# Token sums of x from the channels-first copy: squares, an addition tree and one product with ones

## The chip, the cores and the metric

One NeuronCore of one Trainium2 chip runs the whole program. The metric is the device time of one execution in microseconds. Three runs of the kernel before took 2039.52, 2042.97 and 2034.0 us; their median is 2039.52 us.

## What is computed

The program is a two-layer encoder trunk on 256 tokens of 2048 channels, all in f32. Each layer normalises its input, multiplies it by one wide matrix, runs four branches on the columns of that product, gates and merges them, and adds the result to the input:

```python
def _rms_norm(t, g):
    tf = t.astype(jnp.float32)
    y = tf * lax.rsqrt(jnp.mean(tf * tf, axis=-1, keepdims=True) + NORM_EPS)
    return (y * g.astype(jnp.float32)).astype(t.dtype)
...
    for l in range(DEPTH):
        h = _rms_norm(x, norm_g[l])
        p = h @ w_in[l]
...
        mem_n = _rms_norm(mem, mem_norm_g[l])
        y_d = _mem_attention(m_q, mem_n, mem_w_kv[l], mem_qk_g[l])
...
        x = x + z @ w_out[l]
```

What matters here is the first line of layer 0: every token of x needs the factor (mean of its squared channels + 1e-6) to the power -1/2, and no product of h with w_in can begin before it.

## The kernel before

**Products.** Every weight matrix is streamed from the chip's memory in pieces of two 128-row blocks, 512 KB, into the tile `raww` (three buffers). Each row block of a piece is split into two parts of fewer bits, `whi` (a copy on ScalarE) and `wlo` (the difference, on VectorE), five buffers each; activations are split likewise into `S` (memory, layer by layer), or `T1h` and `T1l` (the normalised x). Each product on TensorE is the sum of high times high, low times high and high times low. The function `product` (line 602) issues them; all matmuls have line 156 and all ScalarE and VectorE instructions line 95, since helpers record them, so they are told apart by their tiles.

**The order of the work.** `main` (line 542) goes through a fixed list of jobs. In layer 0 the first two are the products of the memory tokens with `mem_w_kv` (tiles `S` times `whi`/`wlo`; results `raw` and `V`), the third is the first product of h with `w_in` (`T1h`/`T1l` times `whi`/`wlo`). Beside it run lanes, generators that are given a turn by a running estimate of each engine's time: `norms`, `prep`, `xs`, the `tables` of positions, and the branches. A scheduler of the compiler then sets the order on each engine by its own estimate of durations and by priorities; `issue_after(...)` adds an order between two instructions. Each engine executes its list strictly in order.

**The opening.** Memory arrives channels-first (`memT`, eight pieces of 256 KB into `U` and `ygh`) on ScalarE's DMA queue, the weights on SyncE's. `tick` (line 213) holds a transfer back: it writes one column of its target on GpSimd behind the i-th memset of a row of memsets (`ticks`, lines 190 to 209, each 0.5 us), and the transfer has to wait for that write.

**x in layer 0.** `x_first` (line 401) waits for the last split of memory. It fetches x twice: channels-first (`xT`, four pieces of 512 KB into the freed `U` and `ygh`), and, in `token_sums` (line 381), tokens-first (`in_x`, two pieces of 1 MB into `Z`). From `Z`, ScalarE takes four sums of squares of 1024 channels each, with the sum kept per token (128 tokens on the partitions, so one or two numbers per partition). `rsqrt` (line 176) then raises 128x2 numbers to the power -0.5 on GpSimd. VectorE spreads each over 128 columns (`sq`), and two transposes on TensorE, through the bank `pa`, turn that into a row per token that is the same in all partitions; ScalarE copies it to `r4` (printed as `r`). VectorE multiplies each of 16 channel blocks by the gain and by `r4`, and ScalarE and VectorE split the results into `T1h` and `T1l`. The same `token_sums` serves the memory tokens afterwards (`mrs`); that stays.

Of the kernel before, what the change touches and what calls it, by code (L numbers as in the profile page):

```python
# [15 lines left out]
AF = mybir.ActivationFunctionType  # L16
ALU = mybir.AluOpType
# [4 lines left out]
L, D, S, BW = 2, 2048, 256, 512  # L22
KT = D // 128
EPS = 1e-6
# [12 lines left out]
HP = 2000  # L37
# [8 lines left out]
XE = 5.0  # L46
# [66 lines left out]
class Builder:  # L113
# [230 lines left out]
    def mem_prep(self, l):  # L344

        nc, a = self.nc, self.a
        T = [self.t(f"S{i}", [128, 4, 256], F32R) for i in range(8)]
        X3 = self.t("U", [128, 3, 4, 256])
        X = [X3[:, j] for j in range(3)] + [self.t("ygh", [128, 4, 256])]
        q = nc.scalar if l == 0 else nc.sync  # L350
        g = self.t("gains", [128, 32])
        with self.tc.high_priority(2 * HP):
            nc.sync.dma_start(g, a["gcols"][l])
        self.v["mT", l] = T
        self.v["gains", l] = g
        mem = a["memT"]

        def load(i):
            dst = X[i // 2][:, i % 2 * 2:i % 2 * 2 + 2]
            if not l and i in (1, 2, 3):  # L360
                self.tick((0, 1, 4, 7)[i], dst[:, 0, 0:1])
            q.dma_start(dst, mem[:, 2 * i:2 * i + 2])

        for i in range(8 if l else 4):
            load(i)
        self.ev.add(("mload", l))
        for i in range(8):
            if not l and 1 <= i <= 4:
                with self.tc.issue_after(self.last[0]):
                    load(i + 3)  # L370
            if not l and i == 3:
                with self.tc.issue_after(self.fetch):
                    nc.sync.dma_start(self.cst, a["consts"])
            for kk in (2 * i, 2 * i + 1):
                j, k = kk // 4, kk % 4
                with self.tc.high_priority(2 * HP if kk < 4 else 0):
                    self.split(T[j][:, k], T[4 + j][:, k], X[j][:, k], scale=g[:, kk:kk + 1])
                self.ev.add(("mT", l, kk))
            yield 0.0
# [21 lines left out]
    def x_first(self):  # L401

        nc, a = self.nc, self.a
        yield from self.until(("mT", 0, 15))
        X3 = self.t("U", [128, 3, 4, 256])
        X = [X3[:, j] for j in range(3)] + [self.t("ygh", [128, 4, 256])]
        for j in range(4):
            with self.tc.issue_after(self.last[0]):
                nc.scalar.dma_start(X[j], a["xT"][:, 4 * j:4 * j + 4])
        rs = self.small(2)  # L410
        yield from self.token_sums(a["x"][0], rs)
        ex = self.t("sq", [128, 2, 128])
        nc.vector.tensor_copy(ex, rs[:, :, None].to_broadcast([128, 2, 128]))
        ps = self.pa()[:, :256]
        for tt in range(2):
            self.tr(ps[:, tt * 128:tt * 128 + 128], ex[:, tt])
        rb = self.t("r4", [128, 256], bufs=1)
        self.copy(rb, ps)
        yield
        g = self.v["gains", 0][:, 16:32]  # L420
        hi = self.t("T1h", [128, 16, 256], F32R)
        lo = self.t("T1l", [128, 16, 256], F32R)
        for j in range(8):
            xs = X[j // 2][:, j % 2 * 2:j % 2 * 2 + 2]
            for k in range(2):
                with self.tc.issue_after(self.last[1]):
                    nc.vector.scalar_tensor_tensor(xs[:, k], xs[:, k], g[:, 2 * j + k:2 * j + k + 1], rb,
                                                   op0=ALU.mult, op1=ALU.mult)
            self.split(hi[:, 2 * j:2 * j + 2], lo[:, 2 * j:2 * j + 2], xs)
            yield  # L430
        self.v["hT", 0] = (hi, lo)
        self.ev.add(("hT", 0))
        mrs = self.t("mrs", [128, 2])
        yield from self.token_sums(a["mem"][0], mrs)
        self.v["mrs"] = mrs
        self.ev.add("mrs")
# [105 lines left out]
    def main(self):  # L542
        nc = self.nc
        jobs = [j for l in range(L) for j in self.jobs(l)]
        chunks = [(j, k0, min(2, j.nk - k0)) for j in jobs for k0 in range(0, j.nk, 2)]
        flat = [(i, k) for i, (j, k0, n) in enumerate(chunks) for k in range(n)]
        raws, parts = {}, {}
        nxt = [0]

        def prepare(upto):  # L550
            while nxt[0] < len(flat) and nxt[0] <= upto:
                i, k = flat[nxt[0]]
                j, k0, n = chunks[i]
                w = j.ncol
                if k == 0:
                    raw = self.t("raww", [128, 2, 512], bufs=3)
                    with self.tc.high_priority(HP):
                        for q, (b, e) in enumerate(((0, 1), (1, 2)) if i < 3 else ((0, n),)):
                            if 2 * i + q in (1, 2, 3, 4, 5):
                                self.tick((0, 0, 3, 4, 5, 6)[2 * i + q], raw[:, q, 0:1])  # L560
                            with self.tc.issue_after(self.fetch) if 0 < i < 5 else nullcontext():
                                self.fetch = nc.sync.dma_start(
                                    raw[:, b:e, :w], j.src.rearrange("(k p) n -> p k n", p=128)
                                    [:, k0 + b:k0 + e, j.c0:j.c0 + w]).ins
                    raws[i] = raw
                hi = self.t("whi", [128, 512], F32R, bufs=self.LOOK)
                lo = self.t("wlo", [128, 512], F32R, bufs=self.LOOK)
                with self.tc.high_priority(HP):
                    self.last = self.split(hi[:, :w], lo[:, :w], raws[i][:, k, :w])
                parts[i, k] = (hi, lo)  # L570
                nxt[0] += 1

        pos = 0
        for i, (j, k0, n) in enumerate(chunks):
            if k0 == 0:
                if j.ready is not None:
                    yield from self.until(j.ready)
                act = j.act()
                banks = {}
            nb = 2 if not j.tpos else (j.ncol + 255) // 256  # L580
            if i and (k0 == 0 or k0 + n == j.nk):
                order = [[(k, b) for k in range(n)] for b in range(nb)]
            else:
                order = [[(k, b) for b in range(nb)] for k in range(n)]
            for step in order:
                for k, b in step:
                    kk = k0 + k
                    prepare(pos + k + self.LOOK - 1)
                    if j.kready is not None:
                        yield from self.until(j.kready(kk))  # L590
                        if kk == j.nk - 1:
                            yield from self.until(j.kready(j.nk))
                    if b not in banks:
                        banks[b] = self.bank("mm", 4)
                    self.product(j, kk, b, banks[b], parts[i, k], act(kk))
                    if kk == j.nk - 1:
                        with self.tc.high_priority(HP):
                            j.evac(b, banks[b])
                yield
            pos += n  # L600
# [947 lines left out]
```

## Time and profile before

| | |
|---|---|
| median of three runs | 2039.52 us (2034.0 to 2042.97) |
| profiled execution | 2035.4 us, of which its span 2033.5 us |
| TensorE busy in the span | 2016.3 us (99%) |
| VectorE, ScalarE, GpSimd busy | 1417.8, 1118.1, 152.9 us |
| TensorE matmuls | 12066 |
| moved | 369.45 MB, mean 182 GB/s |

The profile is that of one execution; its times count from the start of the span. Busy times of TensorE are those of pipelined matmuls. A time in square brackets behind a row of the timeline is how long the engine sat idle before it, and which instruction ended that.

### The profile page before, as it was taken

How to read it: one execution, taken by the hardware profiler on the slowest of the kernel's cores; microseconds unless marked ns; L12 is line 12 of the kernel's file. 1: busy time of each engine (PE TensorE's matmuls, PEld its weight loads, DVE VectorE, ACT ScalarE, POOL GpSimd, SP SyncE). 2: the span in 40 equal slices, each digit the busy share in tenths (PEclk: the TensorE clock that was granted, in tenths of full speed). 3: DMA queues.
4: the chain of work that ended last, by engine and by line, in shares of the span. 5: the costliest groups of instructions: out<-in, count | busy, mean ns of one | idle time of the engine just before them, and what ended most of it. 6: DMA issues, size and time to landing. Idle time of an engine off the chain costs nothing.

```text
span 2033.5 us, 33805 instructions
## 1 busy us (share of the span) xinstructions
PE 2016.3 (99%) x12066; PEld 1695.8 (83%) x12066; DVE 1417.8 (70%) x3070; ACT 1118.1 (55%) x2317; POOL 152.9 (8%) x174
## 2 busy tenths in 40 slices
PE   8999999999999999999999999999999999999999
PEld 6998997887877888777889988888778778877887
DVE  5878888986587577558565658666656876765664
ACT  5756565655455445446465556765555554444543
POOL 1201100210010000000000010110011001000000
PEclk9999999999999999999999999999999999999999
DMA  8665655566455556656765656455555555665565
GB/s 298 215 183 157 189 173 171 148 186 186 141 181 165 169 171 191 198 171 226 237 191 179 182 156 179 147 164 175 161 181 166 176 157 158 197 200 165 183 201 190
DMA packets 222585, 369.45 MB, mean 182 GB/s; under 512 B 40592, under 2 KB 60816, under 8 KB 221840
## 3 DMA queue, kind: packets, MB, share of 16 engines
q1 hardware_dynamic: 218736, 356.31, 57.8%
q10 hardware_dynamic: 3456, 10.49, 1.3%
q8 instruction: 95, 1.56, 0.3%
q0 software_dynamic: 224, 0.49, 0.2%
q14 instruction: 74, 0.61, 0.1%
HBM read 359.88 MB, written 11.53 MB: 183 GB/s over the span
## 4 chain that ended last, share of the span: by engine, by line
PE 91%; issue 3%; DVE 2%; DMA 2%; ACT 1%; SPq 0%; POOL 0%; ACTq 0%; DVEq 0%; POOLq 0%
PE mm L156 81%; PE pr L156 5%; PE pa L156 3%; PE pa L161 2%; DMA raww<-in_mem_w_kv 1%; DVE wlo L95 1%; PE pr L161 0%; DVE S L95 0%; DMA raww<-in_w_in 0%; DMA U<-in_memT 0%; ACT whi L95 0%; SPq L1375 0%; DVE Z L95 0%; DVE BK L95 0%; POOL small L179 0%
## 5 line engine op out<-in xcount | busy, mean ns | idle before, releaser
L95 ACT ACTIVATE whi<-raww 128x512 fp32r<-128x512 f32 (+2 forms) x1300 | 786.7, 616 | 738.3 <-PE mm L156 407.0
L95 DVE TENSOR_TENSOR wlo<-raww,whi 128x512 fp32r<-128x512 f32 (+2 forms) x1300 | 863.9, 675 | 449.7 <-ACT whi L95 439.2
L156 PE MATMUL mm<-wlo,T1h 128*128 128x512 f32 (+2 forms) x1440 | 564.6, 392 | 2.6 <-DVE wlo L95 2.6
L156 PE MATMUL mm<-whi,T1l 128*128 128x512 f32 (+2 forms) x1472 | 566.1, 388 | 0.0
L156 PE MATMUL mm<-whi,T1h 128*128 128x512 f32 (+2 forms) x1472 | 537.7, 391 | 1.3 <-ACT whi L95 1.2
L156 PEld LDWEIGHTS mm<-whi,T1h 128*128 128x128 f32 x1472 | 275.3, 188 | 57.1 <-ACT whi L95 2.1
L156 PEld LDWEIGHTS mm<-whi,T1l 128*128 128x128 f32 x1472 | 276.5, 188 | 51.8 <-issue 0.3
L156 PEld LDWEIGHTS mm<-wlo,T1h 128*128 128x128 f32 x1440 | 270.6, 188 | 57.8 <-DVE wlo L95 5.1
L156 PE MATMUL mm<-T1l,whi 128*128 128x256 f32 x960 | 272.4, 285 | 0.4 <-DVE T1l L95 0.4
L156 PE MATMUL mm<-T1h,wlo 128*128 128x256 f32 x960 | 272.6, 286 | 0.0
L156 PE MATMUL mm<-T1h,whi 128*128 128x256 f32 x960 | 272.5, 285 | 0.0
L156 PEld LDWEIGHTS mm<-T1l,whi 128*128 128x128 f32 x960 | 183.6, 191 | 1.6 <-DVE T1l L95 0.6
L156 PEld LDWEIGHTS mm<-T1h,whi 128*128 128x128 f32 x960 | 183.6, 192 | 1.2
L156 PEld LDWEIGHTS mm<-T1h,wlo 128*128 128x128 f32 x960 | 183.0, 191 | 0.8
L156 PE MATMUL mm<-wlo,ygh 128*128 128x512 f32 (+1 forms) x296 | 116.5, 396 | 0.0
L156 PE MATMUL mm<-whi,ygl 128*128 128x512 f32 (+1 forms) x296 | 115.6, 393 | 0.0
L156 PE MATMUL mm<-whi,ygh 128*128 128x512 f32 (+1 forms) x296 | 110.0, 395 | 0.0
L156 PE MATMUL mm<-whi,S 128*128 128x512 f32 x256 | 86.5, 414 | 5.0 <-ACT whi L95 4.8
L179 POOL TENSOR_TENSOR small<-small,cst 128x4 f32<-128x4 f32 (+3 forms) x46 | 52.3, 1139 | 514.1 <-DVE small L95 430.1
L156 PEld LDWEIGHTS mm<-whi,ygl 128*128 128x128 f32 x296 | 55.6, 188 | 12.3 <-issue 1.0
L156 PEld LDWEIGHTS mm<-whi,S 128*128 128x128 f32 x256 | 50.0, 198 | 19.1 <-ACT whi L95 7.6
L156 PEld LDWEIGHTS mm<-whi,ygh 128*128 128x128 f32 x296 | 55.6, 188 | 12.3 <-issue 1.0
(279 smaller groups left out, 2165.8 us busy)
## 6 DMA issues: line engine op xcount, KB each, us to landing
raww<-in_w_in SPq DMA_DIRECT2D x432, 512.0 KB, 3.6
raww<-in_w_branch SPq DMA_DIRECT2D x64, 512.0 KB, 4.5
raww<-in_w_out SPq DMA_DIRECT2D x64, 512.0 KB, 4.6
raww<-in_mem_w_kv SPq DMA_DIRECT2D x29, 512.0 KB, 3.6
raww<-in_w_in SPq DMA_DIRECT2D x16, 384.0 KB, 3.6
raww<-in_w_in SPq DMA_DIRECT2D x16, 320.0 KB, 3.7
raww<-in_w_in SPq DMA_DIRECT2D x16, 256.0 KB, 2.8
Z<-in_x ACTq DMA_DIRECT2D x2, 1024.0 KB, 6.9
```

The lines of the kernel that those rows point to most:

```text
L95: return g(out, *args, **kw)
L156: return self.nc.tensor.matmul(out, lhsT=lhsT, rhs=rhs, start=start, stop=stop).ins
L161: self.nc.tensor.transpose(out, in_, self.ident[:k, :k])
L179: self.nc.gpsimd.tensor_tensor(ss, ss, self.cst[:, C_MH:C_MH + n], op=ALU.pow)
```

## The change

The tokens-first fetch of x is taken out. ScalarE squares the four channels-first pieces (128x1024 each) into the tile `T1l`, which is not yet in use; VectorE adds pieces 0 and 1, 2 and 3, the two results, and then halves the row twice, until 128x256 is left: for each token a sum over 16 channels in each partition. One f32 product with a 128x128 matrix of ones (tile `Rs`) adds the 128 partitions and leaves in every partition the same row of 256 sums. VectorE scales it and adds the small constant (128x256), and GpSimd raises all 128x256 numbers to the power -0.5, with a tile `sq` that is filled with -0.5 as the exponent. The spreading copy and the two transposes go.

The releases by `tick` move: the second to fourth memory piece from steps 1, 4, 7 to 0, 3, 6, and four of the early weight pieces by one step. Fewer splits of memory have the raised priority in layer 0.

```diff
@@ mem_prep
-                self.tick((0, 1, 4, 7)[i], dst[:, 0, 0:1])
+                self.tick((0, 0, 3, 6)[i], dst[:, 0, 0:1])
...
-                with self.tc.high_priority(2 * HP if kk < 4 else 0):
+                with self.tc.high_priority(2 * HP if kk < (4 if l else 2) else 0):
@@ x_first
-        rs = self.small(2)
-        yield from self.token_sums(a["x"][0], rs)
-        ex = self.t("sq", [128, 2, 128])
-        nc.vector.tensor_copy(ex, rs[:, :, None].to_broadcast([128, 2, 128]))
+
+        sq = self.t("T1l", [128, 4, 1024])
+        one = self.t("Rs", [128, 128], bufs=2)
+        nc.gpsimd.memset(one, 1.0)
+        yield XE
+        for j in range(4):
+            with self.tc.issue_after(self.last[0]):
+                nc.scalar.activation(sq[:, j], X[j].rearrange("p k t -> p (k t)"), AF.Square)
+            if j % 2:
+                with self.tc.issue_after(self.last[1]):
+                    nc.vector.tensor_tensor(sq[:, j - 1], sq[:, j - 1], sq[:, j], op=ALU.add)
+            yield
+        nc.vector.tensor_tensor(sq[:, 0], sq[:, 0], sq[:, 2], op=ALU.add)
+        nc.vector.tensor_tensor(sq[:, 0, 0:512], sq[:, 0, 0:512], sq[:, 0, 512:1024], op=ALU.add)
+        nc.vector.tensor_tensor(sq[:, 0, 0:256], sq[:, 0, 0:256], sq[:, 0, 256:512], op=ALU.add)
         ps = self.pa()[:, :256]
-        for tt in range(2):
-            self.tr(ps[:, tt * 128:tt * 128 + 128], ex[:, tt])
+        self.mm(ps, one, sq[:, 0, 0:256])
         rb = self.t("r4", [128, 256], bufs=1)
-        self.copy(rb, ps)
+        nc.vector.tensor_scalar(rb, ps, 1.0 / D, EPS, op0=ALU.mult, op1=ALU.add)
+        half = self.t("sq", [128, 256])
+        nc.gpsimd.memset(half, -0.5)
+        nc.gpsimd.tensor_tensor(rb, rb, half, op=ALU.pow)
         yield
@@ main, prepare
-                                self.tick((0, 0, 3, 4, 5, 6)[2 * i + q], raw[:, q, 0:1])
+                                self.tick((0, 0, 2, 3, 4, 5)[2 * i + q], raw[:, q, 0:1])
```

The scheduler also moves instructions. On TensorE, at the end of the second product with `mem_w_kv` (bank `mm_403` before, `mm_401` now; `S_8` and `S_12` are the last blocks of memory), stood before:

```order
L156 MATMUL mm_403<-whi_496,S_8_98 128x512
L161 MATMUL pa_489<-cst,sq_487 128x128 x2
L156 MATMUL mm_391<-wlo_497,S_8_98 128x512
...
L156 MATMUL mm_403<-wlo_535,S_8_98 128x512
L156 MATMUL mm_403<-whi_534,S_12_102 128x512
L156 MATMUL mm_649<-T1h_516,whi_550 128x256
L156 MATMUL mm_675<-T1h_516,whi_550 128x256
L156 MATMUL mm_649<-T1l_517,whi_550 128x256
```

and now stands:

```order
L156 MATMUL mm_401<-wlo_534,S_8_98 128x512
L156 MATMUL mm_401<-whi_533,S_12_102 128x512
L156 MATMUL pa_486<-T1l_302,Rs_303 128x256
L156 MATMUL mm_648<-T1h_527,whi_545 128x256
L156 MATMUL mm_674<-T1h_527,whi_545 128x256
L156 MATMUL mm_648<-T1l_528,whi_545 128x256
```

The transposes stood 22 matmuls before the first product with `T1h`; the product with ones stands directly before it, and the third matmul behind it reads `T1l`.

On VectorE, from the end of the token sums to the first `T1l`, stood before (`E` belongs to the tables of positions):

```order
L95 SCALAR_TENSOR_TENSOR U_296<-U_296,gains_105,r_103_492 128x256 x4
L95 SCALAR_TENSOR_TENSOR E_626<-E_626 128x64
L95 TENSOR_TENSOR wlo_561<-raww_548,whi_560 128x512
L95 SCALAR_TENSOR_TENSOR U_296<-U_296,gains_105,r_103_492 128x256 x2
L95 TENSOR_TENSOR wlo_577<-raww_574,whi_576 128x512
L95 TENSOR_SCALAR E_626<-E_626 128x64
L95 TENSOR_TENSOR T1l_517<-U_296,T1h_516 128x512 x2
```

and now stands:

```order
L95 TENSOR_TENSOR T1l_302<-T1l_302 128x256
L95 TENSOR_TENSOR wlo_546<-raww_543,whi_545 128x512
L95 TENSOR_TENSOR wlo_560<-raww_543,whi_559 128x512
L95 TENSOR_TENSOR wlo_572<-raww_569,whi_571 128x512
L95 TENSOR_TENSOR wlo_579<-raww_569,whi_578 128x512
L95 TENSOR_SCALAR r_101_488<-pa_486 128x256
L95 TENSOR_TENSOR wlo_645<-raww_642,whi_644 128x512
L95 SCALAR_TENSOR_TENSOR U_296<-U_296,gains_105,r_101_488 128x256 x12
L95 SCALAR_TENSOR_TENSOR ygh_297<-ygh_297,gains_105,r_101_488 128x256 x4
L95 TENSOR_TENSOR T1l_528<-U_296,T1h_527 128x512 x6
```

The first `T1l` came behind 6 of the 16 multiplications by `r4`; it now comes behind all 16.

On GpSimd, behind the fetch of the gains of the rotary part, stood before:

```order
L246 DMA kkn_449<-in_mla_rope_g 128x128
L179 ISA
L179 TENSOR_TENSOR small_302<-small_302,cst 128x2
L254 TENSOR_TENSOR ropeg_666<-cs,kkn_449 128x2x32 x8
L179 TENSOR_TENSOR mrs_619<-mrs_619,cst 128x2
```

and now stands:

```order
L246 DMA kkn_447<-in_mla_rope_g 128x128
L254 ISA
L254 TENSOR_TENSOR ropeg_665<-cs,kkn_447 128x2x32 x8
L431 TENSOR_TENSOR r_101_488<-r_101_488,sq_490 128x256
L179 TENSOR_TENSOR mrs_618<-mrs_618,cst 128x2
```

The power of 128x2 numbers is replaced by one of 128x256, and it now stands behind the eight products of the rotary tables.

## Rows read from the trace of the kernel before

**Rows 1.** The page, part 1 (busy time) and part 4 (chain of work).

```profile
PE 2016.3 (99%) x12066; PEld 1695.8 (83%) x12066; DVE 1417.8 (70%) x3070; ACT 1118.1 (55%) x2317; POOL 152.9 (8%) x174
...
PE 91%; issue 3%; DVE 2%; DMA 2%; ACT 1%; SPq 0%; POOL 0%; ACTq 0%; DVEq 0%; POOLq 0%
```

**Rows 2.** Stretches: us, busy of PE, PEld, DVE, ACT, POOL; granted clock; DMA share, GB/s.

```profile
32.00:38.00 6.00, 3.97 (x17) 2.63 (x15) 1.39 (x3) 2.99 (x6) 0.00 (x0) 1.00 1.05 415
38.00:43.00 5.00, 3.38 (x13) 2.15 (x14) 1.35 (x3) 2.25 (x5) 0.00 (x0) 1.00 1.01 395
43.00:50.00 7.00, 7.00 (x23) 5.26 (x24) 5.64 (x15) 6.80 (x13) 0.75 (x1) 0.76 0.57 186
...
72.00:140.00 68.00, 68.00 (x569) 67.90 (x569) 57.49 (x111) 44.60 (x102) 11.62 (x12) 1.00 0.57 169
```

**Rows 3.** Chain of waits, 0 to 130 us: start us, us, what.

```profile
29.95 12.22 DMA raww<-in_mem_w_kv
```

**Rows 4.** DMA issues, 24 to 44 us: total, then KB each, median us to landing.

```profile
DMA packets 2538, 7.43 MB, mean 371 GB/s; under 512 B 204, under 2 KB 204, under 8 KB 2279
...
Z<-in_x ACTq DMA_DIRECT2D x2, 1024.0 KB, 6.9
U<-in_xT ACTq DMA_DIRECT2D x3, 512.0 KB, 8.4
```

**Rows 5.** Timeline of TensorE: start us, us, instruction, [idle before].

```profile
9.07 1.22 PE L156 MATMUL mm<-whi,S 128*128 128x512 f32 x2 [0.52 <-ACT whi L95]
...
42.87 0.74 PE L156 MATMUL mm<-whi,S 128*128 128x512 f32 x2 [1.62 <-ACT whi L95]
...
56.42 0.38 PE L161 MATMUL pa<-cst,sq 128*128 128x128 f32 x2
...
61.76 0.40 PE L156 MATMUL mm<-T1h,whi 128*128 128x256 f32 x2
62.10 0.39 PE L156 MATMUL mm<-T1l,whi 128*128 128x256 f32 x1
...
68.47 0.39 PE L156 MATMUL mm<-T1l,whi 128*128 128x256 f32 x1 [0.36 <-DVE T1l L95]
```

**Rows 6.** Timeline of ScalarE in the opening.

```profile
33.56 0.63 ACT L95 ACTIVATE whi<-raww 128x512 fp32r<-128x512 f32 x1 [3.65 <-DMA raww<-in_mem_w_kv]
...
38.30 1.04 ACT L95 ACTIVATE Z<-Z 128x1024 f32<-128x1024 f32 x1
```

**Rows 7.** Timeline of GpSimd: single powers of 8, 2, 1 and 4 columns.

```profile
472.40 1.64 POOL L179 TENSOR_TENSOR small<-small,cst 128x8 f32<-128x8 f32 x1 [20.57 <-DVE small L95]
...
614.94 0.70 POOL L179 TENSOR_TENSOR small<-small,cst 128x2 f32<-128x2 f32 x1 [12.42 <-DVE small L95]
...
1266.80 0.56 POOL L179 TENSOR_TENSOR small<-small,cst 128x1 f32<-128x1 f32 x1 [16.08 <-DVE small L95]
1280.95 1.01 POOL L179 TENSOR_TENSOR small<-small,cst 128x4 f32<-128x4 f32 x1 [13.59 <-DVE small L95]
```

**Rows 8.** Groups of GpSimd by shape: busy us, mean ns of one, idle before.

```profile
L179 POOL TENSOR_TENSOR small<-small,cst 128x4 f32<-128x4 f32 x20 | 21.5, 1077 | 126.6 <-DVE small L95 126.6
L179 POOL TENSOR_TENSOR small<-small,cst 128x8 f32<-128x8 f32 x8 | 16.2, 2025 | 114.1 <-ACT jk L95 62.9 <-DVE small L95 49.4 <-ACT PT L95 1.8
```

**Rows 9.** Timeline of GpSimd: the old power of x, and a multiplication of 256 columns.

```profile
49.20 0.75 POOL L179 TENSOR_TENSOR small<-small,cst 128x2 f32<-128x2 f32 x1 [35.22 <-DVE small L95]
...
753.73 0.78 POOL L1195 TENSOR_TENSOR kds<-kds,r 128x256 f32<-128x256 f32 x1 [16.34 <-DVE r L95]
```

**Rows 10.** Timeline of VectorE: multiplications by `r4` and the first `T1l`.

```profile
61.36 1.29 DVE L95 TENSOR_TENSOR T1l<-U,T1h 128x512 fp32r<-128x512 f32 x2
...
63.17 2.46 DVE L95 SCALAR_TENSOR_TENSOR U<-U,gains,r 128x256 f32<-128x256 f32 x6
```

**Rows 11.** Groups of VectorE by shape, 40 to 110 us.

```profile
L95 DVE TENSOR_SCALAR jk<-E 128x256 f32<-128x256 f32 x4 | 1.4, 360 | 0.0
```

**Rows 12.** Groups of TensorE by shape: f32 products of 256 columns.

```profile
L156 PE MATMUL pr<-LA,aup 128*128 128x256 f32 x32 | 9.5, 379 | 0.0
```

## The prediction

> **What bounds the kernel now.** I read the page first, then the table of stretches for the first 140 us, then the timelines of the engines there. TensorE is busy for 99% of the span and carries 91% of the chain that ended last [rows 1]; from 72 us on it has no gap over whole stretches [rows 2]. So TensorE's list is the bound, and the change is worth what it takes from or adds to TensorE's idle time around the start of layer 0. Nothing later catches such time up: a TensorE that stands still for 10 us at 57 us ends 10 us later.
>
> The opening is another stage. From 32 to 43 us TensorE idles 2.03 + 1.62 = 3.65 us while the DMA engines are full, at about 400 GB/s [rows 2]. What ends the waits is a weight piece of the memory product: the chain follows one for 12.22 us [rows 3], ScalarE waits 3.65 us for one before it can split it [rows 6], and TensorE waits 1.62 us in turn [rows 5]. Afterwards the granted clock averages 0.76 over 7 us [rows 2], a mixture of the levels 1.2 and 2.4 GHz, which loses 0.24 x 7 = 1.7 us of work. From 24 to 44 us 7.43 MB are moved, of which the tokens-first x is two transfers of 1 MB [rows 4]. The squares of x take 1.04 us each and lie beside TensorE's work [rows 6].
>
> **The fetch that goes.** 2.1 MB at 371 GB/s [rows 4] are 5.7 us of full DMA engines, more than the 3.65 us of idle time. I take both the idle time and the lost clock as gone: -3.65 and -1.7 us. At the other end they all stay, since the pieces also queue among themselves: 0.
>
> **The tree.** Four squares stay four, of the same size. Five additions on VectorE, the largest 1024 columns, come beside TensorE's second memory product; VectorE is not full there, and its last addition stands ahead of splits that TensorE uses before it reaches the product with ones. Nothing on the path. If that cover were gone, the last addition of 256 columns would add about as much as a multiplication of 256 columns, 2.46/6 = 0.41 us [rows 10].
>
> **The product and what hangs behind it.** Before, the transposes ran at 56.42 us, 5.3 us before the first product with `T1h` at 61.76 [rows 5], and the spreading and half of the multiplications hid behind those 5.3 us. Now the product with ones stands directly ahead of that first product. TensorE has nothing else in its list, so everything between is idle time of TensorE. Step by step:
>
> - Start of the product: 61.76 - 3.65 - 1.7 - 0.38 for the transposes that go [rows 5] = 56.0 us.
> - The product, two passes of 0.38 [rows 12]: 0.76.
> - VectorE's scaling of 128x256: 0.36, as for such an instruction from the on-chip memory [rows 11].
> - GpSimd's power of 128x256. The trace has no power wider than 8 columns. Undisturbed ones take 0.56, 0.70, 1.01 and 1.64 us for 1, 2, 4 and 8 columns [rows 7]: 0.14 to 0.16 us for each further column, with no flattening. From 2 to 8 columns it is 0.94/6 = 0.157 us, so 256 columns are an estimated 1.64 + 248 x 0.157 = 40.5 us. This is the largest term. Bounds: below, a multiplication of 256 columns on GpSimd took 0.78 us [rows 9]; above, the means of the groups, which hold disturbed ones, rise by (2025 - 1077)/4 = 237 ns per column [rows 8], which gives 60.8 us. I take 40.5: the rows are of the same operation, and the engine that disturbs it, VectorE, has nothing to do meanwhile.
> - All 16 multiplications by `r4`, since the first `T1l` now stands behind all of them: 16 x 0.41 = 6.56 [rows 10].
> - The first `T1l`, half of 1.29: 0.65 [rows 10].
>
> Sum 48.8 us; `T1l` is ready at 104.8, where its first reader ran at 62.10 [rows 5]: +42.7 us. The next seven `T1l` come every 0.6 us, faster than TensorE uses them, so the wait of 0.36 us at 68.47 [rows 5] goes. After so long a stop TensorE starts at the lower clock; I take the 1.7 us that the stop at 42.87 was followed by. **42.7 - 0.4 + 1.7 = +44.0 us.**
>
> The Trainium skill speaks against this reading. Its page GPSIMD Engine Reference, section 3.1, puts a two-input elementwise instruction there at about 2.6 cycles per element of a partition; at its 1.2 GHz that is an estimated 0.55 us for 256 columns. The multiplication of 0.78 us agrees [rows 9]; the powers do not [rows 7], and with 0.55 in place of 40.5 the change would be about +4 us.
>
> **Queues.** On GpSimd the power now stands behind eight rotary products. They wait for a table that VectorE's new order has ahead of the second memory product's first split, over 15 us before; eight of them are done by then. Behind the power waits the power of the memory sums, whose readers are ScalarE's scalings of the memory results; they move with the rest. On ScalarE the `T1h` copies and the next weight splits queue behind the wait; on SyncE the weight pieces stop once three buffers are full. All of that idles along with TensorE and costs nothing more. The releases by `tick` come one memset, 0.5 us, earlier; TensorE's idle time of 0.52 us at 9.07 [rows 5] may shrink or grow by that. I put it at 0, between -1 and +1.
>
> **From one execution to the median.** The profiled execution took 2035.4 us, so the sum gives 2079.4. It lies 4.1 us under the median of the runs; the mean of the three runs and of this one is 2038.0, and 2038.0 + 44.0 = **2082 us** is the forecast. A measurement of this kernel can tell about 0.5%, 10 us, from no change.
>
> **Rivals.**
>
> 1. *The power is cheap* (0.78 us, like the multiplication [rows 9], and as the page of the Trainium skill would have it). Then the idle time between the product and `T1l` is 9.1 us and the sum +4.3: 2042 us, no change where I forecast slower. It decides if the power takes under 40.5 - (44.0 - 10.2) = 6.7 us, that is 0.024 us per column. For it: a long instruction may be worked off in blocks that 8 columns do not fill. Against it: then 1, 2, 4 and 8 columns should cost nearly the same, and they don't [rows 7]. Chance 0.12; in 0.02 of it the opening gains so much more that the time is faster by over 0.5%.
> 2. *The opening gains nothing* (the weights stay late, because the earlier releases and the four x pieces of 512 KB, 8.4 us each [rows 4], fill the queue anyway). The power costs 40.5 and the 5.3 us stay: 2087 us. For it: ScalarE's waits are for weights, not for x [rows 6]. Against it: the engines are full, and 2.1 of 7.43 MB go. Chance 0.10.
> 3. *The power is dearer*, 60.8 us by the means [rows 8]: 2102 us. Against it: disturbed powers only. Chance 0.06.
>
> **How the numbers follow.** The forecast has 0.72. The low end takes the smallest step between widths, 0.14 us from 1 to 2 columns (0.70 + 254 x 0.14 = 36.3, -4.2), no loss of clock (-1.7) and a run like the lowest (-4): 2072, and 2071 with the early releases at their best. The high end takes rival 2 (+5.3), a run like the highest (+5) and some more at the lower clock: 2095. That leaves out rivals 1 and 3, 0.18 together. Slower by over 0.5%: 0.72 + 0.10 + 0.06 = 0.88; within: 0.10; faster: 0.02.
>
> **What would show it.** GpSimd has one instruction on 128x256 from `r` and `sq` to `r`, starting near 57 us, of about 40 us; TensorE stands still between the product with ones and the first `T1l` for about 48 us, then runs at the lower clock for a few us; the idle time from 32 to 43 us is gone and the product with ones starts near 56 us; from there to the end the stretches are as before, only later. The prediction is wrong if the power takes under 7 us, or if TensorE has other matmuls to run during it.

## The result, and the profile after

The changed kernel takes 2095.88 us (median of 4 runs, 2093.14 to 2097.06), the kernel before beside it 2038.22 us (4 runs): a ratio of 1.028, 95% interval 1.0255 to 1.0306. It is slower by 57.7 us, where 44 were forecast; the range ended at 2095. The profiled execution took 2095.46 us, its span 2093.7 us.

The page of the changed kernel, parts 1 and 4, against [rows 1]:

```profile
PE 2029.8 (97%) x12066; PEld 1689.9 (81%) x12066; DVE 1426.0 (68%) x3072; ACT 1120.6 (54%) x2312; POOL 184.9 (9%) x176
...
PE 88%; DMA 3%; DVE 3%; POOL 2%; issue 2%; ACT 1%; SPq 0%; DVEq 0%; ACTq 0%; POOLq 0%
```

GpSimd is busy 32 us more and appears in the chain with 2%. TensorE is busy for 97% of a longer span; its busy time, too, has grown, by 13.5 us with the same number of matmuls.

Stretches of the changed kernel (columns as in [rows 2]):

```profile
32.00:43.00 11.00, 9.68 (x41) 7.27 (x40) 9.16 (x18) 8.90 (x14) 1.64 (x5) 1.00 0.71 263
43.00:55.60 12.60, 12.60 (x55) 10.19 (x55) 9.73 (x15) 6.31 (x12) 0.00 (x0) 1.00 0.79 239
62.00:97.00 35.00, 0.00 (x0) 0.00 (x0) 0.00 (x0) 0.00 (x0) 35.00 (x1) 0.50 0.03 13
...
105.00:110.00 5.00, 4.88 (x23) 4.88 (x24) 4.83 (x9) 0.76 (x2) 0.00 (x0) 0.50 0.04 7
110.00:116.00 6.00, 6.00 (x49) 6.00 (x49) 2.81 (x5) 4.09 (x7) 0.00 (x0) 0.94 0.55 168
```

From 32 to 43 us the idle time of TensorE is 1.3 us in place of 3.65 [rows 2], and the clock stays at the full level afterwards. From 62 to 97 us one GpSimd instruction runs and nothing else does. After the stop the granted clock is 0.50 until about 110 us.

TensorE's timeline (as [rows 5]), then the chain of waits through the stop:

```profile
35.72 0.74 PE L156 MATMUL mm<-whi,S 128*128 128x512 f32 x2 [1.32 <-ACT whi L95]
55.60 0.59 PE L156 MATMUL pa<-T1l,Rs 128*128 128x256 f32 x2
99.64 0.80 PE L156 MATMUL mm<-T1h,whi 128*128 128x256 f32 x2 [43.44 <-ACT T1h L95]
105.12 0.58 PE L156 MATMUL mm<-T1l,whi 128*128 128x256 f32 x1 [4.68 <-DVE T1l L95]
```

```profile
56.74 41.28 POOL r L431
98.02 0.02 issue
98.04 4.84 DVE U L95 x12
102.88 1.58 DVE ygh L95 x4
104.46 0.61 DVE T1l L95
105.07 0.04 issue
105.12 30.95 PE mm L156 x238
```

The product with ones starts at 55.60 (56.0 in the prediction), the power takes 41.3 us (40.5), the first `T1l` is read at 105.12 (104.8). At this point the change has cost 105.12 - 62.10 = 43.0 us. But the cost goes on growing. One power of 128x4 stands once in each of eight head groups; here are the first and the last of them in the kernel before and in the changed one:

```profile
138.20 1.45 POOL L1123 TENSOR_TENSOR small<-small,cst 128x4 f32<-128x4 f32 x1 [44.61 <-DVE small L95]
...
1709.73 1.01 POOL L1123 TENSOR_TENSOR small<-small,cst 128x4 f32<-128x4 f32 x1 [6.84 <-DVE small L95]
```

```profile
182.05 1.45 POOL L1136 TENSOR_TENSOR small<-small,cst 128x4 f32<-128x4 f32 x1 [50.57 <-DVE small L95]
...
1764.36 1.01 POOL L1136 TENSOR_TENSOR small<-small,cst 128x4 f32<-128x4 f32 x1 [6.77 <-DVE small L95]
```

The distance is 43.9 us at the first, 54.6 at the last, 60.2 at the ends of the spans. Some 16 to 17 us come after the stop, in small pieces. TensorE waits no more than before there, but is busy for longer. Here is the stretch from the first `T1l` to its last matmuls, before and after (columns as in [rows 2]):

```profile
62.10:2028.00 1965.90, 1959.11 (x11859) 1653.12 (x11859) 1379.78 (x2981) 1081.93 (x2249) 144.02 (x144) 1.00 0.59 179
```

```profile
105.12:2088.00 1982.88, 1976.51 (x11858) 1650.48 (x11859) 1374.87 (x2958) 1078.69 (x2238) 131.37 (x136) 1.00 0.58 176
```

The idle time is 6.8 us before and 6.4 after; the busy time has grown by 17.4 us for the same work, of which the lower clock behind the stop has 2.8 (see below). The groups of matmuls by shape (busy us, mean ns) show the rest, first before, then after:

```profile
L156 PE MATMUL mm<-whi,T1l 128*128 128x512 f32 x1344 | 524.4, 394 | 0.0
...
L156 PE MATMUL mm<-whi,k 128*128 128x512 f32 x64 | 21.6, 396 | 0.0
...
L156 PE MATMUL mm<-whi,q 128*128 128x512 f32 x64 | 21.2, 392 | 0.0
```

```profile
L156 PE MATMUL mm<-whi,T1l 128*128 128x512 f32 x1344 | 530.2, 398 | 0.0
...
L156 PE MATMUL mm<-whi,k 128*128 128x512 f32 x64 | 21.6, 395 | 0.0
...
L156 PE MATMUL mm<-whi,q 128*128 128x512 f32 x64 | 21.2, 392 | 0.0
```

At the same granted clock the matmuls of 512 columns with `T1l` take 4 ns longer, those with `k` and `q` do not. The time from the start of one matmul to the start of the next, called the pitch here, was worked out from all starts of such matmuls in the trace (gaps over 300 ns left out): its median rises from 227 to 234 ns and its mean from 228.3 to 233.1. There are about 4,000 with `T1h` or `T1l`, so 4.8 x 4,000 = 19 us. The 2,880 of 256 columns, which read `T1h` and `T1l` as the moving operand, get faster, from a median of 120 to 117 ns; by the means (123 to 121.5) that is some 5 us. Together +14 us.

What differs is where the tiles lie. The changed `x_first` asks for `T1l` before all others and for `Rs` early, so that the allocation shifts: within 512 bytes of a partition, `T1h`, `T1l` and `V1` start at 0x1a0 (bytes, hexadecimal) in the kernel before and at 0x180, 32 bytes lower, in the changed one. `whi` and `wlo` start at 0x1a0 in both. These places are read off the built programs, no profile shows them; whether they are the cause was for the runs.

### The profile page after: what moved, and what is told of

Its sections match the earlier page's. It is cut to its first block, busy times and chain, and to the rows that moved or that the text cites. A ratio compares the mean times of both kernels' runs of the same rounds, so it can differ in the third digit from the quotient of the medians.

```text
span 2093.7 us, 33802 instructions
## 1 busy us (share of the span) xinstructions
PE 2029.8 (97%) x12066; PEld 1689.9 (81%) x12066; DVE 1426.0 (68%) x3072; ACT 1120.6 (54%) x2312; POOL 184.9 (9%) x176
## 4 chain that ended last, share of the span: by engine, by line
PE 88%; DMA 3%; DVE 3%; POOL 2%; issue 2%; ACT 1%; SPq 0%; DVEq 0%; ACTq 0%; POOLq 0%
PE mm L156 79%; PE pr L156 5%; PE pa L156 3%; POOL r L431 2%; PE pa L161 2%; DVE wlo L95 1%; DMA sp<-sc 1%; DMA sc<-S 1%; DVE S L95 1%; DMA U<-in_memT 1%; PE pr L161 0%; DMA raww<-in_w_in 0%; ACT whi L95 0%; DMA raww<-in_mem_w_kv 0%; DVE Z L95 0%
## 5 line engine op out<-in xcount | busy, mean ns | idle before, releaser
L156 PE MATMUL mm<-whi,T1l 128*128 128x512 f32 (+2 forms) x1472 | 572.0, 392 | 0.0
L156 PE MATMUL mm<-whi,T1h 128*128 128x512 f32 (+2 forms) x1472 | 543.8, 395 | 1.2 <-ACT whi L95 1.2
L156 PEld LDWEIGHTS mm<-wlo,ygh 128*128 128x128 f32 x296 | 55.7, 188 | 12.2 <-issue 0.7
```

What stands on the lines that cost most here:

```text
L156: return self.nc.tensor.matmul(out, lhsT=lhsT, rhs=rhs, start=start, stop=stop).ins
```

## The experiments

**The places of the tiles put back.** Two unused tiles, nothing else:

```diff
@@ x_first
+        self.t("pada", [128, 8])
         sq = self.t("T1l", [128, 4, 1024])
@@ tables
+        self.t("padb", [128, 120])
         ang = self.t("E", [128, 512], bufs=2)
```

> The changed kernel with two unused tiles in between, of 32 and 480 bytes per partition, so that T1h, T1l and V1 start again at the same place within 512 bytes as in the kernel before (0x1a0 in place of 0x180); every instruction stands in the same order on every engine. Theory 1 (the place of these tiles sets the pitch of the matmuls that read them as the stationary operand): the 512-column matmuls with T1h and T1l go back from 234 to 227 ns from start to start, and the time falls by 15 to 17 us to 2079 to 2081 us; the power still takes 41 us. Theory 2 (the drift after 140 us comes from the scheduler's new order, or is the difference between two executions): the time stays at 2094 to 2098 us and the pitch at 234 ns.

It took 2084.18 us (4 runs), 1.0211 times the kernel before beside it (1.019 to 1.0232; that one took 2041.48 here). The power still takes 41.27 us. The same two instructions of the head groups, then the group of matmuls:

```profile
181.20 1.45 POOL L1138 TENSOR_TENSOR small<-small,cst 128x4 f32<-128x4 f32 x1 [51.27 <-DVE small L95]
...
1754.52 1.01 POOL L1138 TENSOR_TENSOR small<-small,cst 128x4 f32<-128x4 f32 x1 [6.84 <-DVE small L95]
```

```profile
L156 PE MATMUL mm<-whi,T1l 128*128 128x512 f32 x1344 | 525.0, 394 | 0.0
```

The mean is 394 ns again (the pitch 227), and the distance to the kernel before is 43.0 us at the first group, 44.8 at the last and 46.7 at the ends of the spans: most of the growth is gone. In the ratio it is 0.7% of the time, some 14 us; against the changed kernel's median it is 11.7, since this kernel ran beside runs that were 3 us longer. Either is less than the 15 to 17 expected. Theory 2, which had the time unchanged, falls.

**The change's places given to the kernel before.**

```diff
@@ x_first
         self.copy(rb, ps)
+        self.t("pada", [128, 120])
@@ tables
+        self.t("padb", [128, 8])
         ang = self.t("E", [128, 512], bufs=2)
```

> The kernel before with two unused tiles of 480 and 32 bytes per partition, so that T1h, T1l and V1 start at 0x180 within 512 bytes as in the changed kernel, and all else as before; every instruction stands in the same order. Theory 1: the pitch of the 512-column matmuls with T1h and T1l rises from 227 to 234 ns and the time by 15 to 17 us, to 2053 to 2055 us. Theory 2: the time stays at 2034 to 2043 us, the pitch at 227 ns.

2053.31 us (5 runs), a ratio of 1.0062 (1.0043 to 1.0082), beside the same 2041.48: 12 to 13 us for two unused tiles. That is less than the 15 to 17 expected; I think I had left out part of what the 256-column matmuls give back (their median is 117 ns here), but no run shows that alone.

```profile
L156 PE MATMUL mm<-whi,T1l 128*128 128x512 f32 x1344 | 530.1, 398 | 0.0
```

**Which place counts.** In the kernel before, `whi`, `wlo` and `raww` alone moved by 32 bytes:

```diff
@@ main, prepare
+                    if i == 0:
+                        self.t("pad0", [128, 8])
                     raw = self.t("raww", [128, 2, 512], bufs=3)
@@ params
+        if l == 0:
+            self.t("pad1", [128, 120])
         cols = self.t("cols", [128, P_N + 29])
```

> The kernel before with raww, whi and wlo moved by 32 bytes (whi and wlo start at 0x1c0 within 512 bytes in place of 0x1a0), T1h, T1l, V1 and all other tiles at the places they had within 512 bytes; every instruction in the same order. Theory 1a (what counts is the distance between the two operands of a matmul; it is then that of the changed kernel, 0x20): the 512-column matmuls with T1h and T1l take 234 ns from start to start, those of 256 columns 117, and the time rises by about 12 us to 2050 to 2056 us. Theory 1b (the place of the stationary operand alone counts): the 512-column ones stay at 227 ns and the time within 5 us of the kernel before's.

2053.12 us (4 runs), ratio 1.006 (1.0045 to 1.0075), where the kernel before took 2041.19.

```profile
L156 PE MATMUL mm<-whi,T1l 128*128 128x512 f32 x1344 | 530.2, 398 | 0.0
...
L156 PE MATMUL mm<-whi,q 128*128 128x512 f32 x64 | 21.5, 396 | 0.0
...
L156 PE MATMUL mm<-whi,k 128*128 128x512 f32 x64 | 21.3, 392 | 0.0
```

`T1l` and `q`, which lie where they lay, became slow, and `k` became fast, though it did not move either. So the distance between the two operands counts (theory 1a), not the place of one. It is that of the changed kernel: `T1l` starts 32 bytes below `whi`. `k` starts at 0xc0, `whi` now at 0x1c0: for `k`, 256 bytes apart is as good as 0.

**All stationary tiles at distance 0.** In the kernel before, three unused tiles bring `S0` to `S7`, `X`, `ygh` (0x120 before), `ygl`, `k1` and `iA` (0xc0) to 0x1a0:

```diff
@@ setup
+        self.t("pad0", [128, 32])
         pace = self.t("X", [128, 1024])
@@ tables
+        self.t("pad1", [128, 96])
         pp = self.t("q1", [128, 1024], I32)
...
+        self.t("padb", [128, 56])
         ang = self.t("E", [128, 512], bufs=2)
```

> The kernel before with unused tiles in between, so that every tile that a 512-column matmul reads as the stationary operand (S0 to S7, X, ygh, ygl, k1, iA beside T1h, T1l, V1, q1) starts at 0x1a0 within 512 bytes, as whi and wlo do; every instruction in the same order. Both forms of theory 1: the matmuls with S, X, ygh, ygl, k and iA, some 1,500 that take 230 to 233 ns, come down to about 227 to 228, and the time falls by 5 to 8 us to 2030 to 2034 us. Rival (only T1h, T1l and V1 are sensitive, or ygl and ygh take 231 ns for another reason): the time stays within 2 us of the kernel before's.

2037.46 us (12 runs) against 2041.19 (26 runs), ratio 0.9979 (0.9969 to 0.9989): 4.3 us faster by the ratio, a little under the forecast 5 to 8 and more than the rival's 2.

```profile
L156 PE MATMUL mm<-whi,k 128*128 128x512 f32 x64 | 21.3, 391 | 0.0
L156 PE MATMUL mm<-whi,q 128*128 128x512 f32 x64 | 21.1, 391 | 0.0
L156 PE MATMUL mm<-whi,X 128*128 128x512 f32 x64 | 20.9, 391 | 0.0
```

**The power alone.** The changed kernel with the power of 2 columns in place of 256:

```diff
-        nc.gpsimd.tensor_tensor(rb, rb, half, op=ALU.pow)
+        nc.gpsimd.tensor_tensor(rb[:, 0:2], rb[:, 0:2], half[:, 0:2], op=ALU.pow)
```

> The changed kernel with the power taken of 2 of the 256 columns alone; the other 254 columns of the factor are left without it. The order of the instructions is the same but for that one. Theory 1 (the power is the stall): it takes 0.7 us in place of 41.3, TensorE waits 7 to 9 us between the product with ones and the first T1l, and the time falls by 40 to 42 us to 2054 to 2056 us. Rival (another instruction, such as the 16 multiplications or a late weight piece, would hold TensorE anyway): the time falls by less than 30 us.

2055.99 us (4 runs): 39.9 us under the changed kernel's median, and 1.0072 times the kernel before (1.0048 to 1.0096), where the changed kernel is at 1.028; by the ratios that is 42 us. GpSimd, then TensorE:

```profile
57.01 0.72 POOL L431 TENSOR_TENSOR r<-r,sq 128x2 f32<-128x2 f32 x1 [22.20 <-DVE r L95]
```

```profile
59.63 0.50 PE L156 MATMUL mm<-T1h,whi 128*128 128x256 f32 x2 [3.16 <-ACT T1h L95]
65.11 0.58 PE L156 MATMUL mm<-T1l,whi 128*128 128x256 f32 x1 [4.99 <-DVE T1l L95]
```

The power was the stop: the first `T1l` is read at 65.11 in place of 105.12 us. What is left of it, 3.16 + 4.99 us, is the chain of the other steps between the product with ones and the first `T1l`.

**The releases.** The changed kernel with the old steps and the old priority, first in a single execution, then in four:

```diff
-                self.tick((0, 0, 3, 6)[i], dst[:, 0, 0:1])
+                self.tick((0, 1, 4, 7)[i], dst[:, 0, 0:1])
@@ main, prepare
-                                self.tick((0, 0, 2, 3, 4, 5)[2 * i + q], raw[:, q, 0:1])
+                                self.tick((0, 0, 3, 4, 5, 6)[2 * i + q], raw[:, q, 0:1])
@@ mem_prep
-                with self.tc.high_priority(2 * HP if kk < (4 if l else 2) else 0):
+                with self.tc.high_priority(2 * HP if kk < 4 else 0):
```

> The changed kernel with the releases at their old steps and the old priority of the splits of memory, the rest as in the change. Theory 1 (the opening is faster because the tokens-first x is gone): the idle time of TensorE from 32 to 43 us stays near 1.3 us, the product with ones starts within 1 us of 55.6 us, and the time is within 2 us of the changed kernel's. Rival (the earlier releases gave the 5 us): the product starts at 58 us or later.

> The changed kernel with the old releases and the old priority once more, timed in rounds. If the look before holds (product with ones at 59.0 in place of 55.6 us), it starts after 58 us again and the time is 3 to 4 us over the changed kernel's 2095.9, 2098 to 2101 us; if that was the accident of one execution, it starts near 56 us and the time is within 2 us of 2096.

The product with ones started at 59.03 us in the first trace and at 58.55 in the second, so 3 us later than in the change, both times:

```profile
58.55 0.59 PE L156 MATMUL pa<-T1l,Rs 128*128 128x256 f32 x2
```

The idle time from 32 to 43 us did not stay near 1.3: it is 2.7 and 1.9 us. Yet the time of the four runs is 2095.43 us, a ratio of 1.028 (1.0263 to 1.0297), as for the change (the single execution had given 2099.69). The expectation that 3 us in the opening are 3 us at the end did not hold here.

And the new releases alone in the kernel before, the same three lines the other way round:

> The kernel before with the new releases and the new priority of the memory splits alone; x still comes twice. Theory 1 (the idle time from 32 to 43 us is the DMA engines' and goes with the tokens-first x alone): the first product with T1h starts within 1 us of 61.8 us, the idle time from 32 to 43 us stays over 3 us, and the time within 4 us of the kernel before's. Rival (the earlier releases gave 3 us or more, as the look at the change without them would say): the first product with T1h starts at 59 us or earlier and the time falls by 3 us or more.

2038.17 us (10 runs) against 2038.18, ratio 0.9998 (0.9985 to 1.001): nothing. In its timeline the first `T1h` product comes 3.2 us earlier than in [rows 5], at 58.55, but waits for the next operand, so that at the first `T1l` 1.3 us are left of them:

```profile
58.55 0.39 PE L156 MATMUL mm<-T1h,whi 128*128 128x256 f32 x2
60.77 0.39 PE L156 MATMUL mm<-T1l,whi 128*128 128x256 f32 x1 [1.82 <-DVE T1l L95]
```

The two parts of the change can now be taken apart, by the start of the first instruction behind the products of memory: 61.76 us before; 58.55 with the new releases and priority alone; 58.55 and 59.03 without the tokens-first fetch alone; 55.60 with both. So each has about 3 of the 6.2 us, and the rival named the size of the first share rightly.

Where these 3 us arise is less clear. With the new releases alone TensorE still idles 3.1 us from 32 to 43 us, with x fetched twice, as the first theory had it. It has started 97 matmuls of the memory products by 32 us, where it had started 94 before (some 0.7 us), and 127 by 43 us, where it had started 121 (1.4 us). The other 1.7 us are the lower clock, which the kernel before had from 43 to 50 us [rows 2] and this one did not:

```profile
43.00:50.00 7.00, 7.00 (x32) 5.68 (x31) 5.31 (x18) 6.12 (x12) 0.75 (x1) 1.00 0.67 200
```

These are traces of one execution each. In the time of the whole kernel neither run shows the 3 us. Later waits differ by more: from the first `T1l` on TensorE idles 6.8 us in the trace of the kernel before, 14.1 in that of the kernel with the new releases alone, 6.4 in that of the change and 4.6 in that of the change with the old releases.

**The change mended.** x still comes only channels-first, with squares and tree as in the change. The product has the tree's halves as the stationary operand, so that the sums lie by token and the power is narrow; two issue orders hold the product and the transposes ahead of TensorE's last memory blocks, and a third brings the first `T1l` forward. The additions, the steps behind them and the first four multiplications also get a raised priority, and an unused tile brings `T1l` to 0x1a0 (both left out below):

```diff
@@ x_first
-        self.mm(ps, one, sq[:, 0, 0:256])
...
+            for tt in range(2):
+                self.gate13 = self.mm(ps[:, 2 * tt:2 * tt + 2], sq[:, 0, tt * 128:tt * 128 + 128], self.ones)
+            rs = self.small(4)
+            nc.vector.tensor_scalar(rs, ps[:, 0:4], 1.0 / D, EPS, op0=ALU.mult, op1=ALU.add)
+            nc.gpsimd.tensor_tensor(rs, rs, self.cst[:, C_MH:C_MH + 4], op=ALU.pow)
+            ex = self.t("sq", [128, 2, 128])
+            nc.vector.tensor_copy(ex, rs.rearrange("p (a b) -> p a b", b=2)[:, :, 0:1].to_broadcast([128, 2, 128]))
+            ps = self.pa()[:, :256]
+            for tt in range(2):
+                self.gate15 = self.tr(ps[:, tt * 128:tt * 128 + 128], ex[:, tt])
...
+                    with self.tc.issue_after(lows[j - 2]) if j > 1 else nullcontext():
...
@@ main
+                    if 8 <= i < 16 and kk == 13:
+                        gate = self.gate13
+                    if i == 15 and kk == 15:
+                        gate = self.gate15
+                    with self.tc.issue_after(gate) if gate else nullcontext():
+                        self.product(j, kk, b, banks[b], parts[i, k], act(kk))
```

> The change mended: x only channels-first, squares and tree as in the change; the product now has the tree's 128x128 halves as the stationary operand and two columns of ones, so that the sums lie by token, GpSimd's power is of 128x4, and spreading, two transposes and the copy are those of before; the product is held ahead of block 13 and the transposes ahead of block 15 of the second memory product, and the first T1l comes behind 4 of the 16 multiplications; T1h, T1l and V1 at 0x1a0. Theory 1: the power takes 1.0 us, TensorE waits under 4 us before the first T1l, which is read at 58 to 61 us in place of 62.1, and the time is 1 to 5 us under the kernel before's, 2034 to 2038. Rival (the waits only move, to the product with ones or the transposes): no faster than before.

2037.39 us (10 runs), ratio 0.9981 (0.9972 to 0.9991) beside 2041.19, so 3.9 us by the ratio:

```profile
59.51 0.51 PE L156 MATMUL mm<-T1h,whi 128*128 128x256 f32 x2 [1.72 <-ACT T1h L95]
60.69 0.39 PE L156 MATMUL mm<-T1l,whi 128*128 128x256 f32 x1 [0.68 <-DVE T1l L95]
```

TensorE waits 2.4 us, and `T1l` is read 1.4 us earlier than before. The second version has the stationary tiles at 0x1a0 too, by unused tiles as above:

> The mended change with all stationary tiles at 0x1a0 as well. Theory 1: both gains add up, 7 to 12 us under the kernel before, 2026 to 2032 us.

2034.26 us (9 runs), ratio 0.9972 (0.996 to 0.9984): 5.7 us under the kernel before by the ratio, the fastest of the kernels here, though under the 7 to 12 expected. The two gains alone were 4.3 and 3.9 us; the interval, 3.3 to 8.2 us, does not exclude that they add up. In the one profile `T1l` is read only at 62.64 us, later than in the first version; whether that is so in every execution no run shows.

## Why the prediction was right or wrong

**The opening and the stop** came at the times predicted. The steps stand at 55.60 us (56.0), 41.3 us for the power (40.5, from four powers of up to 8 columns [rows 7]) and 105.12 us (104.8). The power's 41.27 us are 161 ns per column; the run with 2 columns gave 40 to 42 us back, so it is shown, not argued, that it was the cost. Rival 1 falls with it. The page GPSIMD Engine Reference of the Trainium skill, section 3.1, falls as a price for this operation: its 2.6 cycles per element, there for an add, give an estimated 0.55 us, near the multiplication's 0.78 us [rows 9] and some 75 times less than the power took.

**The start of the product with ones** came out right by luck. Up to there 5.7 us were booked, 3.65 + 1.7 for the fetch that goes and 0.38 for the transposes, and 6.2 came. But the runs give the fetch and the transposes only about 3 us, and the other 3 to the releases and the priority, which I had put at 0: two terms were wrong, and the errors made each other up. Of the idle time from 32 to 43 us, which I took as gone, 1.3 us stayed.

**The lower clock** after the stop was booked with 1.7 us. It lasted from 105.1 to about 110.4 us at half speed, which loses 0.5 x 4.9 + 0.06 x 6 = 2.8 us. So 48 us of idle time were followed by a dearer start than 1.62 us had been.

**The step that failed** is the last one: "from there to the end the stretches are as before, only later", and with it the missing term of the sum. They are later and slower: TensorE's 512-column matmuls with `T1h`, `T1l` and `V1` went from 227 to 234 ns, as the first tiles that the change asks for moved these by 32 bytes against `whi` and `wlo`. I counted instructions added and removed, and took their durations as given. The sum had nothing for it; the runs size it at 0.7% between the changed kernel and the same with the tiles put back, and 0.6% between the kernel before and the same with its tiles moved, 12 to 14 us. With it taken out, the change costs 2.11% (1.9 to 2.32), 43 us on 2038; the prediction said 44.0. The sentence "Nothing later catches such time up" is not borne out for small shifts either: the change with the old releases reads its first `T1l` 2.9 us later than the change, at 108.06 us, and its profiled span is the same 2093.7 us.

**Rivals 2 and 3** didn't come: the product with ones was not late, and the power kept to its undisturbed price per column. VectorE was not busy beside it (0.00 us from 62 to 97); that this is why, no run shows.

## What to carry to other kernels

Price an operation from rows of the same operation at two or more widths, and look whether the time grows with the width: four short powers told the price of a wide one to 2%, while the multiplication of the same shape was too low by a factor of 50. Where TensorE is the bound, a change of the order in which tiles are asked for is a change too: compare the places of the operands of its largest groups of matmuls before and after, and keep them fixed with an unused tile when something else is to be measured. And a narrow value per token is best raised to a power while it is narrow, and spread afterwards.

## What the runs showed of the hardware that I had not expected

The pitch of matmuls of 512 columns depends on the distance between the stationary and the moving tile. Here are medians at the full clock, worked out from the starts in the traces of these kernels. The distance is the start of the stationary tile less that of `whi` or `wlo`, modulo 256 bytes (whole steps of 256 taken off), so that 0xe0 is 32 bytes below and 0x20 is 32 bytes above:

```
distance  median ns  tiles and kernels
0x00      227        T1h, T1l, V1, q1 before; k1, iA with whi moved; all tiles when aligned
0x20      230 to 235 ygl, k1, iA before (230 to 232 beside whi, 235 beside wlo)
0x40      231 to 236 k1, iA in the first mended version (231 beside whi, 236 beside wlo)
0x60      234 to 235 S, X with whi moved
0x80      231 to 233 S, X before
0xe0      232 to 235 T1h, T1l, V1 in the change; T1h, T1l, V1, q1 with whi moved
```

Not every group fits. With `whi` moved, `ygl` lies at distance 0 and its matmuls took 231 ns, and `ygh` lies at 0x60 and its took 230 to 231 in place of 234. They follow one another in TensorE's list, but neighbours alone do not explain it, since a `ygh` directly behind a `ygh` came after 228.5 ns (32 times). With all tiles at 0 both took 227. That the distance counts modulo 256 bytes rests on tiles such as `k1` and `iA` with `whi` moved, 256 bytes apart.

For matmuls of 256 columns, where `whi` is the stationary operand and `T1h` or `T1l` the moving one, it is the other way round: 120 ns with both at the same place, 117 to 118 with `T1h` and `T1l` 32 bytes below `whi`. Why the distance counts, no run here shows. Other distances were not tried.
